# Nine pairs of mixer projections by seven block products, and weight remainders by accumulating transfers

## The chip, the cores and the metric

The kernel runs on one core of a Trainium2 chip. The metric is the device time of one execution in microseconds (us). A profiled execution has its own time, and a span from its first to its last instruction. The engines are called as in the profile: PE (TensorE matmul), PEld (its weight loads), DVE (VectorE), ACT (ScalarE), POOL (GpSimd) and SP (SyncE, which issues transfers here).

## The reference

Two post-norm layers over 528 tokens (512 and 16 meta tokens) of 1024 features, all in float32:

```python
def hybrid_mixer(h, w_in, q_norm_g, kv_norm_g, w_uq, w_ukv, w_out, pos, valid):
    proj = h @ w_in
    sb_q, sb_k, sb_v, c_q, c_kv, k_r, r_q, r_k, r_v, r_g = jnp.split(proj, IN_SPLITS, axis=-1)
    out_a = stick_breaking_attention(hs(sb_q, SB_HEADS), hs(sb_k, SB_HEADS), hs(sb_v, SB_HEADS), valid)
    q = (rms_norm(c_q, q_norm_g) @ w_uq) ...
    kv = (rms_norm(c_kv, kv_norm_g) @ w_ukv) ...
    out_b = mla_attention(q_nope, q_rope, k_nope, k_rope, v_b, valid)
    rq, rk = apply_rope(hs(r_q, 4), pos), apply_rope(hs(r_k, 4), pos) * (RET_QK ** -0.5)
    y_c = head_norm(multiscale_retention(rq, rk, hs(r_v, 4))).reshape(B, L, D_RET)
    out_c = silu(r_g) * y_c
    return jnp.concatenate([out_a, out_b, out_c], axis=-1) @ w_out

for l in range(DEPTH):
    mix = hybrid_mixer(h, ...)
    h = layer_norm(DN_ALPHA * h + mix, ln1_g[l], ln1_b[l])
    h = layer_norm(DN_ALPHA * h + jnp.square(jax.nn.relu(h @ w_ff1[l])) @ w_ff2[l], ln2_g[l], ln2_b[l])
```

`w_in` has 30 blocks of 128 output features here: 12 for stick-breaking attention (four head pairs of q, k, v), four for retention's q and k (numbers 12 to 15), eight for its values and gates (16 to 23), and six for the latents of the latent attention (24 to 29, the last the rotary key).

## The kernel before, in words

Features lie on partitions, tokens in columns. Every operand of a matmul is a pair of fp32r tiles: `hi`, the rounded value, and `lo`, the remainder. A product is three matmuls, hi*hi, hi*lo and lo*hi, added up in PSUM (`proj`, L650). A block of 128 outputs over K = 1024 is eight tiles of K, so 24 matmuls for each group of columns. Two groups of columns, 256 and 272, cover 528 tokens; in layer 1, whatever only queries need (retention's q, the gates, the query latents) is one group of 512.

Weights come through `wload` (L536): SP loads 128x512 into one of eight raw tiles (pool `r`), ACT copies it to `hi`, and DVE subtracts to get `lo` (`wsplit`, L549; 14 tiles in pool `w`). The MLP's matmuls use another scheme, `strassen` (L630): two weight blocks and two halves of K form a 2x2 matrix, the two halves of the tokens another, and seven block products of four K tiles each (84 matmuls) give what eight would (96). Its weight side (`strassen_weights`, L558) makes seven split weight tiles, of which two are sums that a transfer adds up while it lands (issued by POOL) and two are sums that DVE adds. Its other side, `strassen_sums` (L593), makes sums of the token halves.

`ret_qk` (L972) projects retention's q and k and applies rotation; `ret_vg` (L1028) makes one head's values and its gate; `mla_c` (L1123) makes the latents and norms them; `mla_proj` (L1186) takes them to heads; `wout_part` (L1320) is one of the 12 pieces of the output projection (group 0 stick-breaking, 1 retention, 2 latent attention).

The order on each engine comes from a planner (`schedule`, L312): every operation is recorded with a rank, and a list scheduler with estimated costs places it on its engine when its operands are due and its tiles are free; the table `PR` holds the ranks. PE gets the matmuls of projections as filler between the steps of the attention chains. The pool `u` holds 75 tiles of 528 columns.

Of the kernel before, what the change touches and what calls it, by code (L numbers as in the profile page):

```python
# [425 lines left out]
class Builder:  # L426
# [109 lines left out]
    def wload(self, src, eng=None):  # L536
# [3 lines left out]
        for c in range(0, n, 512):  # L540
# [4 lines left out]
            hi, lo = self.wsplit(raw, eng)  # L545
# [12 lines left out]
    def strassen_weights(self, src1, src2):  # L558
# [55 lines left out]
    def strassen_inputs(self, a, b, H, i):  # L614
# [13 lines left out]
        return d  # L628

# [94 lines left out]
    def ln_emb(self, h, c0, c1):  # L724
# [6 lines left out]
        self.ln_back(xns, 0, h, c0, c1)  # L731
# [1011 lines left out]
```

## Time and profile before

| | |
|---|---|
| median of 3 runs | 1547.27 us (1546.6 to 1547.67) |
| the profiled execution's own time | 1546.99 us |
| its span | 1545.2 us |
| PE busy | 1504.6 us (97%), 11490 matmuls |
| PEld busy | 1443.6 us (93%) |
| DVE, ACT, POOL busy | 1303.8, 963.7, 197.9 us |
| granted PE clock, mean | 0.995 |

The stages in order of time, by the shapes and places of their instructions: start and first norm until about 30 us; layer 0's stick-breaking attention with its projections 30 to 130; retention and the latents, with the last stick-breaking heads, 130 to 300; latent attention 300 to 410; end of the mixer, norm and the plain part of the MLP 410 to 480; MLP 480 to 770; norm 770 to 810; then layer 1 in the same order, 810 to 905, 905 to 1058, 1058 to 1163, 1163 to 1229, 1229 to 1510, and the last norm and output. All operations are recorded through one helper and have one line, L414, so that groups are told apart by tiles and shapes: `w` weights, `r` raw weights, `u` everything else in SBUF, `ps` PSUM, `t` small statistics.

### The profile page before, as it was taken

What the parts mean: (1) busy time and instruction counts of PE and PEld (TensorE: products, weight loads), DVE (VectorE), ACT (ScalarE), POOL (GpSimd) and SP (SyncE); (2) the same over time, 40 slices, a digit from 0 to 9 for tenths busy, and PEclk for the clock granted to TensorE, in tenths of its full rate; (3) what the DMA queues carried; (4) which work ended last, traced back from release to release, by engine and by line L of the source; (5) the groups of instructions that cost most, each with busy time, mean ns of one, the idle gap of its engine ahead of it and who ended that gap; (6) DMA issues with size and microseconds to landing.
All of it is one profiled execution on the core that took longest, in us unless ns stands there. A gap on an engine that the chain in (4) does not pass through costs nothing.

```text
span 1545.2 us, 31629 instructions
## 1 busy us (share of the span) xinstructions
PE 1504.6 (97%) x11490; PEld 1443.6 (93%) x11490; DVE 1303.8 (84%) x3131; ACT 963.7 (62%) x2263; POOL 197.9 (13%) x309
## 2 busy tenths in 40 slices
PE   6999999999999999999999999999999999999997
PEld 6999999988999999999999999888889899999996
DVE  7778877998789898888877778779987988989896
ACT  5675744578667484757646657446884857666670
POOL 4113100010001111111102112001000011111110
PEclk9999999999999999999999999999999999999999
DMA  5424412321124767677514333424212277777752
GB/s 196 117 78 124 141 62 76 100 81 49 56 83 115 185 165 178 177 181 175 171 56 131 103 91 95 127 76 125 57 62 83 69 190 180 186 183 181 186 154 82
DMA packets 102668, 190.32 MB, mean 123 GB/s; under 512 B 13552, under 2 KB 14832, under 8 KB 102512
## 3 DMA queue, kind: packets, MB, share of 16 engines
q1 hardware_dynamic: 81840, 145.98, 30.0%
q0 software_dynamic: 20672, 42.32, 14.9%
q8 instruction: 90, 1.47, 0.4%
q14 instruction: 66, 0.54, 0.1%
HBM read 167.87 MB, written 2.10 MB: 110 GB/s over the span
## 4 chain that ended last, share of the span: by engine, by line
PE 87%; DVE 9%; ACT 2%; issue 1%; DMA 0%; SPq 0%; DVEq 0%; ACTq 0%
PE ps L414 87%; DVE u L414 6%; ACT u L414 2%; DVE t L414 2%; DVE w L414 1%; DMA u<-in_xm 0%; SPq L414 0%; DVE r L414 0%; ACT w L414 0%; DVEq L1738 0%; ACT t L414 0%; DVEq L414 0%; ACTq L414 0%
## 5 line engine op out<-in xcount | busy, mean ns | idle before, releaser
L414 PE MATMUL ps<-u,w 128*128 128x256 f32 (+3 forms) x9384 | 1281.2, 294 | 14.7 <-DVE u L414 7.6
L414 PEld LDWEIGHTS ps<-u,w 128*128 128x128 f32 x9384 | 1199.7, 189 | 49.7 <-DVE u L414 11.3
L414 ACT CAST w<-r 128x512 fp32r<-128x512 f32 x610 | 364.5, 617 | 293.0 <-PE ps L414 249.2
L414 DVE TENSOR_TENSOR w<-r,w 128x512 fp32r<-128x512 f32 x604 | 404.8, 686 | 59.2 <-ACT w L414 42.9
L414 DVE TENSOR_TENSOR u<-u,u 128x512 fp32r<-128x512 f32 (+10 forms) x541 | 283.3, 548 | 10.8 <-ACT u L414 8.9
L414 DVE TENSOR_TENSOR u<-ps,u 128x256 fp32r<-128x256 f32 (+11 forms) x518 | 198.0, 409 | 48.3 <-ACT u L414 28.8
L414 PE MATMUL ps<-u,u 128*128 128x272 f32 (+5 forms) x1012 | 183.8, 307 | 1.7 <-ACT u L414 0.9
L414 POOL DMA_DIRECT2D r<-in_wff x108 | 94.8, 881 | 652.0 <-DVE u L414 331.4
L414 ACT CAST u<-u 128x512 fp32r<-128x512 f32 (+7 forms) x287 | 149.8, 540 | 39.9 <-DVE u L414 34.7
L414 ACT ACTIVATE u<-u 128x256 f32<-128x256 f32 (+5 forms) x349 | 161.7, 475 | 15.3 <-DVE u L414 12.3
L414 PEld LDWEIGHTS ps<-u,u 128*128 128x128 f32 (+1 forms) x1012 | 150.2, 190 | 8.6 <-ACT u L414 1.4
L414 ACT ACTIVATE u<-ps 128x512 f32<-128x512 f32 (+9 forms) x185 | 88.6, 484 | 89.8 <-PE ps L414 78.6
L414 DVE TENSOR_TENSOR u<-u,ps 128x256 f32<-128x256 f32 (+3 forms) x236 | 98.7, 429 | 43.6 <-PE ps L414 42.3
L414 POOL DMA_DIRECT2D u<-u x112 | 58.0, 523 | 483.7 <-ACT u L414 442.6
L414 PE MATMUL ps<-ident,u 128*128 128x128 f32 x672 | 103.4, 278 | 12.4 <-DVE t L414 9.2
L414 ACT COPY u<-ps 128x256 f32<-128x256 f32 (+6 forms) x186 | 72.1, 395 | 54.3 <-PE ps L414 52.2
L414 PEld LDWEIGHTS ps<-ident,u 128*128 128x128 f32 x672 | 79.7, 142 | 19.1 <-DVE t L414 7.9
L414 ACT CAST u<-ps 128x16 fp32r<-128x16 f32 (+7 forms) x260 | 72.4, 330 | 26.4 <-PE ps L414 15.8
L414 DVE TENSOR_TENSOR r<-r,r 128x512 f32<-128x512 f32 x108 | 74.0, 685 | 2.3 <-DMA r<-in_wff 2.1
L414 DVE SCALAR_TENSOR_TENSOR u<-ps,u 128x512 f32<-128x512 f32 (+7 forms) x73 | 41.6, 579 | 25.5 <-ACT u L414 23.2
L414 ACT ACTIVATE u<-ps,t 128x512 f32<-128x512 f32 (+4 forms) x86 | 48.0, 561 | 16.7 <-DVE t L414 13.5
L414 DVE CAST u<-u 128x256 fp32r<-128x256 f32 (+5 forms) x147 | 49.6, 353 | 8.2 <-ACT u L414 7.7
(57 smaller groups left out, 600.6 us busy)
## 6 DMA issues: line engine op xcount, KB each, us to landing
r<-in_wff SPq DMA_DIRECT2D x310, 256.0 KB, 3.3
r<-in_win SPq DMA_DIRECT2D x120, 256.0 KB, 3.0
r<-in_wff POOLq DMA_DIRECT2D x108, 256.0 KB, 4.8
r<-in_wout SPq DMA_DIRECT2D x48, 256.0 KB, 2.9
u<-u POOLq DMA_DIRECT2D x80, 132.0 KB, 4.0
u<-u SPq DMA_DIRECT2D x48, 66.0 KB, 2.4
u<-in_xm SPq DMA_DIRECT2D x10, 256.0 KB, 5.5
u<-in_dec SPq DMA_DIRECT2D x8, 264.0 KB, 3.5
```

The costliest lines, as they stand in the source:

```text
L414: o.ins = getattr(getattr(nc, o.eng), o.fn)(*[r(x) for x in o.args], **{k: r(x) for k, x in o.kw.items()})
```

## The change

Three things are done. (1) Nine pairs of blocks in each layer (retention's q and k, four heads' value with gate, and three pairs of latents) go through `strassen` in a new `pair_proj`, with halves of 264 tokens in both layers; the token side is made once per layer by `right_factors`, from the unsplit activations `raw`, which are now kept. (2) For the stick-breaking weights of head pairs 1 to 3, `mla_proj`, two groups of the output projection and one of the seven weights of each pair, `lo` is made by `wsplit_dma`: ACT writes the negative rounded weight, and a second transfer, issued by POOL, adds the weight to it. (3) Ranks move: output projection group 0 later, the latents ahead of retention's last heads. `strassen_weights` also loads and splits `a12` before `a11`, in the MLP too.

```diff
-    wo0=(1.6, 1.6), mc=(7.9, 6.8), mp0=(7.4, 7.0), ...
+    wo0=(3.1, 3.1), mc=(6.8, 6.0), mp0=(7.2, 6.8), ... hs=(2, 2), hp=2, ...
+    def wsplit_dma(self, raw, src):
+        hi, lo = self.W.tile([P, n], F32R), self.W.tile([P, n], F32R)
+        with nc.rank(nc.cur + PR['wl']):
+            nc.scalar.activation(lo, raw, AF.Copy, scale=-1.0)
+            nc.gpsimd.dma_start(lo, src.bitcast(F32R), accum_op=ALU.add)
+            nc.scalar.copy(hi, raw)
...
-    def strassen_weights(self, src1, src2):
+    def strassen_weights(self, src1, src2, dma=False):
         load("s1", a21, a22)
+        load("a12", a12)
         load("a11", a11)
-        load("a12", a12)
         w["s1"] = self.wsplit(t["s1"])
+        single = lambda n, src: self.wsplit_dma(t[n], src) if dma else self.wsplit(t[n])
+        w["a12"] = self.wsplit(t["a12"])
         w["a11"] = self.wsplit(t["a11"])
...
-        w["a12"] = self.wsplit(t["a12"])
         w["s3"] = self.wsplit(t["s3"])
-        w["a22"] = self.wsplit(t["a22"])
+        w["a22"] = single("a22", a22)
+    def right_factors(self, h, raw, H, keep=False):
+        for i in range(4):
...
+            self.strassen_sums(raw[i], raw[i + 4], t1[:, o], e[:, :H], t)
+            self.split(th[:, :2 * H], tl[:, :2 * H], t[:, :2 * H], "a")
+            self.split(t2[0][:, o], t2[1][:, o], e[:, :H], "a")
...
+            if keep:
+                self.split(*hs[i]["t1"], t1[:, o], "a")
+    def pair_proj(self, src1, src2, hs):
+        w = self.strassen_weights(src1, src2, True)
+        c1, c2 = self.unit(), self.unit()
+        self.strassen(w, hs, ("z1", "y", "x1", "z2", "x2", "x3", "x4"), H, dict(
+            z1=lambda X, Y, Z: nc.scalar.copy(c2[:, B], Z), y=lambda X, Y, Z: nc.scalar.copy(c1[:, A], Y),
+            x1=lambda X, Y, Z: nc.vector.tensor_add(c1[:, A], X, c1[:, A]),
+            z2=lambda X, Y, Z: nc.scalar.copy(c1[:, B], Z),
+            x2=lambda X, Y, Z: nc.vector.tensor_add(c1[:, B], X, c1[:, B]),
+            x3=lambda X, Y, Z: nc.vector.scalar_tensor_tensor(out=c2[:, B], in0=X, scalar=-1.0, in1=c2[:, B], op0=ALU.mult,
+                                                              op1=ALU.subtract),
+            x4=lambda X, Y, Z: nc.scalar.activation(c2[:, A], X, AF.Copy, scale=-1.0)))
+        return c1, c2
     def sb_weights(self, l, p, ranks=None):
+                ws.append(self.wload(self.a["win"][l, 3 * p + i], (self.nc.gpsimd if i in PR['GW'] else None) if ranks else
+                                     "dma" if p else None))
     def ret_qk(self, l, hs):
-                self.proj(pa[:, :n], wa, 0, h, c0, c1)
-                self.proj(pb[:, :n], wb, 0, h, c0, c1)
+            pa, pb = self.pair_proj(self.a["win"][l, 12 + 2 * which], self.a["win"][l, 13 + 2 * which], hs)
     def ret_vg(self, l, hd, hs):
-        V = last(self.v_tokens(wv, 0, h, 1))
+        v, g = self.pair_proj(self.a["win"][l, 16 + 2 * hd], self.a["win"][l, 17 + 2 * hd], hs)
+        V = self.v_parts(v, 1)
     def mla_c(self, l, hs):
+        ckv = self.pair_proj(win(27), win(28), hs)
+        cq = self.pair_proj(win(24), win(25), hs)
+        c3, kt = self.pair_proj(win(26), win(29), hs)
-                    nc.vector.tensor_copy(cs[i][:, c0:c1], ps[:, :n])
     def mla_proj(self, l, p, cn, kr, tabs):
-        wq = self.wload(self.a["wuq"][l, p])
-        wkv = self.wload(self.a["wukv"][l, p])
+        wq = self.wload(self.a["wuq"][l, p], "dma")
+        wkv = self.wload(self.a["wukv"][l, p], "dma")
     def wout_part(self, l, g, c, mixed, r, h=None):
+        w = self.wload(self.a["wout"][l, g, c], "dma" if g < 2 else None)
     def layer(self, l, h, raw, first):
+            if p == PR['hp']:
+                with nc.rank(R + PR['hs'][l]):
+                    hs = self.right_factors(h, raw, NT // 2, True)
```

How this moves instructions is shown at three places. The first is PE in layer 1, where retention head 2's value and gate are projected. Before, the value is projected alone and group by group (`ps_14338` ends the group of 256 columns, `ps_14390` begins that of 272; `ps_14397` is the attention of head 0):

```order
L414 MATMUL ps_14338<-u_11939,w_14184 128x256
L414 MATMUL ps_14338<-u_11949,w_14184 128x256
L414 MATMUL ps_14338<-u_11939,w_14235 128x256
L414 MATMUL ps_14390<-u_11866,w_14062 128x272
L414 MATMUL ps_14390<-u_11877,w_14062 128x272
L414 MATMUL ps_14397<-u_14378,u_13689 128x144
L414 MATMUL ps_14390<-u_11866,w_14213 128x272
```

Now, at the same head:

```order
L414 MATMUL ps_14707<-u_12024,w_14583 128x264
L414 MATMUL ps_14707<-u_12036,w_14583 128x264
L414 MATMUL ps_14707<-u_12024,w_14596 128x264
L414 MATMUL ps_14707<-u_12079,w_14583 128x264
L414 MATMUL ps_14716<-u_13222,w_14498 128x264
L414 MATMUL ps_14716<-u_13319,w_14498 128x264
L414 MATMUL ps_14716<-u_13222,w_14521 128x264
```

The value and the gate are computed together, by products of 264 columns (`ps_14716` is the product of the first weight sum with a sum of token halves, `ps_14707` that of `a12`), and their weights come from a pair's seven sets.

The second place is DVE in layer 0, where retention's head 0 starts (`r` and `w` rows are weights, `ps` with `u_2647` or `u_2871` the decay of the scores). Before:

```order
L414 TENSOR_TENSOR w_2774<-r_2148,w_2700 128x512
L414 TENSOR_TENSOR u_2604<-ps_2693,u_2740 64x512
L414 TENSOR_TENSOR w_2796<-r_2283,w_2787 128x512
L414 TENSOR_TENSOR u_2815<-u_2604,u_2800 128x528
L414 TENSOR_TENSOR w_2825<-r_2311,w_2807 128x512
L414 TENSOR_TENSOR u_2828<-ps_2805,u_2828 128x128
L414 TENSOR_TENSOR u_2842<-ps_2835,u_2647 128x512
```

Now:

```order
L414 TENSOR_TENSOR w_2890<-r_2691,w_2793 128x512
L414 TENSOR_TENSOR u_2668<-ps_2851,u_2894 64x16
L414 TENSOR_TENSOR u_2858<-ps_2728,u_2858 128x264
L414 TENSOR_TENSOR w_2913<-r_2693,w_2897 128x512
L414 TENSOR_TENSOR w_2922<-r_2720,w_2906 128x512
L414 TENSOR_TENSOR u_2668<-ps_2845,u_2894 64x512
L414 TENSOR_TENSOR r_2935<-r_2693,r_2725 128x512
L414 TENSOR_TENSOR u_2949<-ps_2931,u_2871 128x512
```

Between the same steps of the attention now stand more splits, a weight sum (`r_2935`) and a sum read from PSUM (`u_2858<-ps_2728`).

The third place is POOL in layer 0, behind its set-up, where it copies head pair 0's q and k to the layout of the scores (`u<-u`, 64x528). Before:

```order
L414 CAST rep_434<-u_106 128x128
L414 DMA u_544<-u_313 64x528
L414 DMA u_544<-u_341 64x528
L414 DMA u_577<-u_383 64x528 x2
L414 DMA u_610<-u_313 64x528
L414 DMA u_610<-u_341 64x528
L414 DMA u_644<-u_383 64x528 x2
L414 DMA u_796<-u_656 64x528
```

Now:

```order
L414 CAST rep_434<-u_106 128x128
L414 DMA w_347<-in_win 128x512
L414 DMA w_499<-in_win 128x512
L414 DMA w_523<-in_win 128x512
L414 DMA u_548<-u_313 64x528
L414 DMA u_548<-u_341 64x528
L414 DMA u_578<-u_381 64x528 x2
L414 DMA u_615<-u_313 64x528
L414 DMA u_615<-u_341 64x528
L414 DMA u_646<-u_381 64x528 x2
L414 DMA w_542<-in_win 128x512
L414 DMA w_565<-in_win 128x512
```

Three of head pair 1's `lo` transfers stand ahead of the copies and three behind them, on the one queue of POOL.

## Rows read from the trace of the kernel before

**Rows 1.** The page, parts 1 and 2: engines' busy times, PE by slices.

```profile
PE 1504.6 (97%) x11490; PEld 1443.6 (93%) x11490; DVE 1303.8 (84%) x3131; ACT 963.7 (62%) x2263; POOL 197.9 (13%) x309
...
PE   6999999999999999999999999999999999999997
```

**Rows 2.** The page, part 4: chain that ended last, by engine.

```profile
PE 87%; DVE 9%; ACT 2%; issue 1%; DMA 0%; SPq 0%; DVEq 0%; ACTq 0%
```

**Rows 3.** Stretches: us; PE, PEld, DVE, ACT, POOL busy (instructions); clock, DMA, GB/s.

```profile
30.00:130.00 100.00, 99.46 (x775) 96.81 (x776) 76.91 (x173) 66.92 (x144) 21.34 (x40) 1.00 0.41 108
130.00:300.00 170.00, 169.95 (x1365) 168.11 (x1364) 137.22 (x351) 91.09 (x212) 10.74 (x16) 1.00 0.30 92
300.00:410.00 110.00, 106.57 (x815) 99.42 (x814) 100.89 (x357) 86.93 (x284) 11.24 (x32) 1.00 0.24 70
480.00:770.00 290.00, 283.42 (x2293) 281.09 (x2293) 258.49 (x503) 185.32 (x396) 46.81 (x55) 0.99 0.69 176
...
905.00:1058.00 153.00, 152.98 (x962) 137.92 (x961) 118.36 (x271) 81.03 (x170) 11.47 (x16) 1.00 0.33 98
1058.00:1163.00 105.00, 104.74 (x641) 90.12 (x640) 95.20 (x299) 83.14 (x252) 8.79 (x22) 1.00 0.25 71
1229.00:1510.00 281.00, 276.21 (x2293) 272.98 (x2293) 254.17 (x502) 183.79 (x396) 44.65 (x51) 0.99 0.70 176
```

**Rows 4.** The same view: PE at 264 columns, at 512, and at 256.

```profile
600.00:660.00 60.00, 60.00 (x493) 59.88 (x492) 52.45 (x101) 41.30 (x92) 10.50 (x12) 1.00 0.69 171
1213.00:1228.00 15.00, 15.00 (x67) 12.18 (x66) 14.92 (x38) 12.95 (x28) 0.87 (x1) 1.00 0.28 60
1260.00:1320.00 60.00, 60.00 (x511) 60.00 (x510) 53.20 (x106) 40.45 (x91) 10.97 (x13) 1.00 0.75 189
```

**Rows 5.** Groups by form: xcount, busy us, mean ns, idle before, releasers.

```profile
L414 DVE TENSOR_TENSOR w<-r,w 128x512 fp32r<-128x512 f32 x596 | 401.7, 690 | 59.1 <-ACT w L414 42.9 <-PE ps L414 8.4
L414 ACT CAST w<-r 128x512 fp32r<-128x512 f32 x602 | 361.5, 619 | 292.4 <-PE ps L414 248.7 <-DVE r L414 25.5 <-issue 11.2
...
L414 POOL DMA_DIRECT2D r<-in_wff x108 | 94.8, 881 | 652.0 <-DVE u L414 331.4 <-DVE w L414 110.8 <-DMA r<-in_wff 95.6
...
L414 DVE TENSOR_TENSOR r<-r,r 128x512 f32<-128x512 f32 x108 | 74.0, 685 | 2.3 <-DMA r<-in_wff 2.1
...
L414 POOL DMA_DIRECT2D u<-u x112 | 58.0, 523 | 483.7 <-ACT u L414 442.6 <-PE ps L414 19.6 <-DVE u L414 10.3
...
L414 DVE TENSOR_TENSOR u<-u,u 128x528 fp32r<-128x528 f32 x64 | 45.2, 711 | 2.6 <-ACT u L414 2.5
...
L414 DVE TENSOR_TENSOR u<-ps,u 128x264 f32<-128x264 f32 x39 | 16.7, 429 | 4.0 <-PE ps L414 3.6
...
L414 ACT COPY u<-ps 128x264 f32<-128x264 f32 x39 | 14.4, 370 | 3.2 <-PE ps L414 3.1
```

**Rows 6.** DVE in order of time: start us, us, three splits merged.

```profile
1235.29 1.89 DVE L414 TENSOR_TENSOR w<-r,w 128x512 fp32r<-128x512 f32 x3
```

**Rows 7.** Who waited for whom: us in total, times, longest.

```profile
PE ps L414 <- DVE u L414: 10.9, 16, 2.0
...
ACT w L414 <- DMA r<-in_win: 0.4, 2, 0.3
...
PEld ps L414 <- DVE w L414: 0.4, 2, 0.2
```

**Rows 8.** DMA issues: queue, xcount, KB each, median us to landing.

```profile
r<-in_win SPq DMA_DIRECT2D x120, 256.0 KB, 3.0
r<-in_wff POOLq DMA_DIRECT2D x108, 256.0 KB, 4.8
```

More of the change, by code (lines that the diff above doesn't have):

```diff
@@ L762, in v_tokens, with v_parts @@
                 yield
+        return self.v_parts(vt, heads)
+    def v_parts(self, vt, heads):
+        nc = self.nc
         n = 2 * P
@@ L1334, in wout_group, with accum, layer @@
         self.proj(ps[:, :n], w, 4 * m, mixed, c0, c1)
-        self.accum(ps[:, :n], r[mt][:, c0:c1], h[mt] if g == 0 else None, c0, c1)
-    def accum(self, ps, r, hp, c0, c1):
-        nc = self.nc
-        if hp is None:
-            nc.vector.tensor_add(r, r, ps)
-        else:
-            hi, lo = f32(hp[0][:, c0:c1]), f32(hp[1][:, c0:c1])
-            nc.vector.scalar_tensor_tensor(out=r, in0=hi, scalar=ALPHA, in1=ps, op0=ALU.mult, op1=ALU.add)
-            nc.vector.scalar_tensor_tensor(out=r, in0=lo, scalar=ALPHA, in1=r, op0=ALU.mult, op1=ALU.add)
-    def layer(self, l, h, first):
+        self.accum(ps[:, :n], r[mt][:, c0:c1], [x[:, c0:c1] for x in h[mt]] if h else ())
+    def accum(self, ps, r, h=()):
+        add = ps
+        for x in h:
+            self.nc.vector.scalar_tensor_tensor(out=r, in0=f32(x), scalar=ALPHA, in1=add, op0=ALU.mult, op1=ALU.add)
+            add = r
+        if not h:
+            self.nc.vector.tensor_add(r, r, ps)
+    def layer(self, l, h, raw, first):
         nc = self.nc
@@ L1535, in layer @@
                 ff1(mt, *g)
-        sums = []
-        for i in range(4):
-            if i % 2 == 0:
-                t1 = self.unit()
-                t2 = [self.unit(F32R), self.unit(F32R)]
-            o = slice((i % 2) * H, (i % 2) * H + H)
-            t, e = self.unit(), self.unit()
-            self.strassen_sums(raw[i], raw[i + 4], t1[:, o], e[:, :H], t)
-            th, tl = self.unit(F32R), self.unit(F32R)
-            self.split(th[:, :2 * H], tl[:, :2 * H], t[:, :2 * H], "a")
-            self.split(t2[0][:, o], t2[1][:, o], e[:, :H], "a")
-            (ah, al), (bh, bl) = h[i], h[i + 4]
-            A, B = slice(0, H), slice(H, 2 * H)
-            hs.append(dict(b11=(ah[:, A], al[:, A]), b21=(bh[:, A], bl[:, A]), b22=(bh[:, B], bl[:, B]), t1=(ah[:, B], al[:, B]),
-                           t2=(t2[0][:, o], t2[1][:, o]), t3=(th[:, A], tl[:, A]), t4=(th[:, B], tl[:, B])))
-            sums.append((hs[i]["t1"], t1[:, o]))
-        for (hi, lo), x in sums:
-            self.split(hi, lo, x, "a")
+        hs += self.right_factors(h, raw, H)
         for i in range(npl):
@@ L1577, in layer @@
         hn = None if final else self.new_h()
+        raw = None if final else [self.unit() for _ in range(KT)]
         with nc.rank(R + 31):
-            self.ln_group(r, 2, hn, *gs[0], final)
+            self.ln_group(r, 2, hn, *gs[0], final, raw)
         first = None
@@ L1585, in layer @@
         with nc.rank(R + 33):
[L1586 removed]
+            self.ln_group(r, 2, hn, *gs[1], final, raw)
         self.PP = self.PA
         nc.cur = R + 100
[L1589 removed]
+        return hn, raw, first
     def record(self):
@@ L1596, in record @@
         nc.cur = -2.6
-        self.ln_emb(h, *gs[0])
+        raw = [self.unit() for _ in range(KT)]
+        self.ln_emb(h, *gs[0], raw)
         WR = PR['WR']
@@ L1606, in record @@
         for l in range(DEPTH):
-            h, first = self.layer(l, h, first)
+            h, raw, first = self.layer(l, h, raw, first)
     def build(self):
```

158 lines of the change are left out of this document (74 added, 84 removed).

## Prediction

> **What bounds the kernel now.** I read the page's busy times first. PE is busy 1504.6 of 1545.2 us, in every slice but the first and the last nearly all of it [rows 1], and the chain that ended last runs through PE for 87% [rows 2]. A busy PE need not be a PE at its peak, so the second view is the stretches [rows 3] beside stretches of one shape of matmul [rows 4]. In the MLP 493 matmuls of 264 columns fill 60 us, 0.1217 us each; 511 of 256 columns fill 60 us, 0.1174 us each; 67 of 512 columns fill 15 us, 0.224 us each (a little too low, since those under way at an edge count too). The time follows the columns, 0.46 ns a column at 256 and 264, at a granted clock of 1.00, which is the 2.4 GHz level. What is worth something is therefore fewer columns, as long as nothing keeps PE waiting. In retention with the latents PE hardly waits: 0.05 us in 170, and 0.02 in 153 in layer 1 [rows 3]. DVE is the next engine: 81% and 77% there, 92% in layer 0's latent attention, where PE idles 3.4 us of 110, and 89 to 90% in the MLPs, where PE idles 6.6 of 290 and 4.8 of 281 [rows 3]. These say how much DVE may do before PE feels it.
>
> The sum is made against the profiled execution's own time, 1546.99 us: its span of 1545.2 and 1.8 around it. The median of the runs shown, 1547.27, is 0.02% above, so nothing is added for that. A measurement can tell about 0.2% from no change, 3.1 us: faster means below 1544.2, slower above 1550.4.
>
> **PE columns.** A pair of blocks was 2 x 24 matmuls per column group: with groups of 256 and 272, 48 x 528 = 25,344 columns; with one group of 512, 24,576. It becomes 84 matmuls of 264, 22,176 columns. In layer 0 all nine pairs have the two groups. In layer 1 nine of the 18 blocks do and nine are 512 wide. Together 648 matmuls of 256, 648 of 272 and 216 of 512 go, and 1512 of 264 come: in columns 342,144 + 110,592 - 399,168 = 53,568 fewer. At 0.46 ns that is 24.6 us, 13.1 in layer 0 and 11.5 in layer 1. With the 512-wide ones at their own 0.224 and the 272-wide ones at 0.125 (272 x 0.46 ns), it is 76.1 + 81.0 + 48.4 - 184.0 = 21.5. I take 24, since 0.224 is too low at its edges, and keep 21.5 to 24.6. The number of matmuls, and so of weight loads, stays exactly what it was: 1512 out, 1512 in.
>
> The Trainium skill, Perfetto Trace Analysis, section Identifying the Most-Contended Engine, says that TensorE's room is to be judged by the busy share of its weight loads and not by that of its matmuls; here that is 93%. If weight loads set the pace, an unchanged number of them would give back nothing; the 512-wide row speaks against that, and it is a rival below.
>
> **DVE.** Each of the nine pairs of a layer had four splits on DVE and now has six and two weight sums, so four operations of 128x512 more, and three sums that read 264 columns from PSUM. Their durations are 0.69 and 0.43 us [rows 5], but three splits in a row take 1.89 [rows 6], so 0.60 each and 0.09 of tail that the next one covers. Without tails a pair adds 4 x 0.60 + 3 x 0.34 = 3.4 us, nine 30.8. Eight splits of the output projection leave the same stretch (4.8), and the copies of the latents out of PSUM, ten of about 0.34 in layer 0 (3.4), about as much in layer 1 (four and three wide ones, 3.2). That is +22.6 a layer, on 137.2 in layer 0 and 118.4 in layer 1 [rows 3]. The right factors are four times four sums of 264 columns, one split of 528 (0.71, so 0.62) and two of 264: 10.7 us, due before the first pair, beside the stick-breaking heads, where 18 splits (10.8 us) leave DVE. So they cost nothing there; if they ran late, PE would wait for the first pair only.
>
> In the stretch of retention DVE would then have 160 us of work in 170 - 13 = 157, and 141 in 153 - 11.5 = 141.5. That is an upper bound: busy time holds the tails of instructions that nothing followed, at most 0.09 for each of about 396 and 316 instructions, 36 and 28 us. Its demand lies between 124 and 160 of 157 (79 to 102%), and between 113 and 141 of 141.5 (80 to 100%). The middle, 142 and 127, is 90%, the share of the MLPs and of latent attention. What PE idles at that share is 0.25% (layer 1's latent attention) to 3.1% (layer 0's) [rows 3]. For 298 us that is 0.7 to 9.2 us; I take 1.7%, the lower of the two MLPs, 5 us, since the MLP has this very code with the same 14 weight tiles.
>
> **ACT.** Each pair adds four operations of 128x512 at 0.53 (0.62 less tail) and four copies of 264 columns out of PSUM at 0.28 [rows 5], which take over from copies and squares that read PSUM: 9 x 3.2 = 29 us, and 4 for the output projection, on 91 in layer 0's retention [rows 3]: 124 of 157, 79%. The 18 stick-breaking weights add 9.5 us and the right factors 4.6 to 67 of 100. In latent attention 20 weight tiles add about 10 us to 87, 88% of 110, while DVE loses about 11 of its 101. One engine is relieved and the other loaded, so I count the 3.4 us that PE idles there as unchanged; all of it could go, or as much again come.
>
> **POOL, SP and the transfers.** POOL gets 146 more transfers: 92 for single weights, and for each of 18 pairs one `lo` and two weight sums. At 0.52 to 0.88 us [rows 5] that is 76 to 128 us on an engine that is busy 198 of 1545, and SP issues 18 more. Nothing of it lies on the path, because weights are ready early: ACT waited 0.4 us in all for projection weights to land, and weight loads 0.4 for DVE's splits [rows 7]. A `lo` by transfer comes about 5 us later than by DVE: 4.8 to land [rows 8] and 0.9 to issue, against 0.7. The DMA share of 0.30 in that stretch rises, but the MLP lives with 0.69 [rows 3]. In POOL's queue a transfer that waits for ACT holds up the copies of q and k behind it, and the stick-breaking scores wait for those: cost nothing while ACT is ahead, and else the rival below.
>
> **The latents earlier.** Their norm chain now runs beside retention's last heads and not ahead of latent attention. What it can save is in the 3.4 us above. The order of `a12` and `a11` in the MLP shifts one split by about 0.6 us in a stream that is prepared ahead (the 0.4 us of weight loads behind DVE's splits [rows 7] holds for the MLP too). I count nothing.
>
> **Sum:** 1547.0 - 24 + 5 = **1528 us**. With 24.6, no new idle time and the 3.4 gone it is 1519; with 21.5, 9.2 and 3.4 more it is 1538. Its own range is 1518 to 1535, the sum's ends not all coming together.
>
> **The rivals.** (a) *DVE becomes the bound of retention.* No stretch shows DVE above 92%. At the top of its demand the two stretches last 160/0.92 = 174 and 141/0.92 = 153 us, not 157 and 141.5: 29 us more, 1547 - 24 + 29 = 1552, slower than before. It decides from a demand of 92% on (145 and 130 us); halfway from there to the top it costs 9 and 6 us, 1547 - 24 + 15 = 1538. For it: DVE waits on PE and ACT between the steps of attention, which the MLP has less of. Against it: the right factors and some weights can be made ahead, and the middle of the demand stays below. Chance: 0.17 for a part (1535 to 1544), 0.06 for above that.
>
> (b) *The accumulating transfers come late.* A layer has 30 sets of weights that use them: nine stick-breaking blocks, four second latent projections, eight pieces of the output projection and nine pairs. One that PE must wait for costs up to the 5 us above; eight of them are 40 us: 1547 - 24 + 40 = 1563. It takes six to make the kernel slower. Against it is the 0.4 us of waits [rows 7]; for it, that one queue holds splits and copies together. Chance 0.05.
>
> (c) *Weight loads set the pace*, and 1512 of them for 1512 give nothing: 1547, no change. Against it: one load took 0.224 us of pace at 512 columns and 0.117 at 256 [rows 4]. Chance 0.04.
>
> (d) Below 1518, should the shorter DVE work beside stick-breaking attention and latent attention give more than I see: 0.04.
>
> **How the numbers follow.** Forecast 0.64 (1518 to 1535), (a) 0.17 and 0.06, (b) 0.05, (c) 0.04, (d) 0.04. Faster: 0.64 + 0.17 + 0.04 = 0.85. Above 1544.2, (a) and (b) leave 0.01 each within the bound, so with (c) 0.06 the same, and 0.09 slower. The range 1518 to 1544 holds 0.81.
>
> **What would show it.** Right: 11490 matmuls again and PE busy about 1480; PE idle in retention below 5 us a layer; DVE busy 87 to 95% there and about 1325 in all; POOL busy some 300. Wrong by (a): PE's waits on DVE, 10.9 us now [rows 7], go to 40 and more, in retention. Wrong by (b): weight loads wait for `w` from a transfer. Wrong by (c): the same span with PE's pace at 264 columns as slow as at 272.

## The result, and the profile after

The changed kernel is slower: 1561.94 us, median of four runs (1560.68 to 1567.92), against 1546.93 (1546.33 to 1547.67) for the kernel before in the same comparison. The ratio is 1.0106, with a 95% interval of 1.0089 to 1.0123. Forecast were 1528 and a range up to 1544.

The profiled execution took 1560.68 us, its span 1558.9. The page, parts 1, 2 and 4 (busy times, PE by slices, the chain by engine), against [rows 1] and [rows 2]:

```profile
PE 1495.7 (96%) x11490; PEld 1435.1 (92%) x11490; DVE 1324.1 (85%) x3172; ACT 1061.6 (68%) x2485; POOL 325.7 (21%) x449
...
PE   6999999899999999999999998999999999999997
...
PE 79%; DVE 11%; ACT 3%; DMA 3%; issue 2%; POOL 0%; SPq 0%; DVEq 0%; ACTq 0%; POOLq 0%
```

The work is what was forecast: 11490 matmuls, DVE at 1324.1 us (1325), POOL at 325.7 (some 300). PE's busy time fell by 8.9 us where 24 were due, and its idle time (span less busy) rose from 40.6 to 63.2. The stretches, with the columns of [rows 3]:

```profile
30.00:130.00 100.00, 96.77 (x753) 93.76 (x753) 73.22 (x176) 76.81 (x169) 38.25 (x58) 1.00 0.66 147
130.00:300.00 170.00, 164.17 (x1279) 158.52 (x1277) 151.26 (x363) 119.62 (x268) 44.97 (x54) 1.00 0.72 171
300.00:410.00 110.00, 104.80 (x773) 96.44 (x772) 94.33 (x334) 89.18 (x282) 22.67 (x45) 0.97 0.43 99
480.00:770.00 290.00, 285.34 (x2309) 283.15 (x2308) 261.80 (x510) 189.81 (x407) 46.19 (x55) 0.99 0.69 173
905.00:1058.00 153.00, 145.88 (x1044) 137.87 (x1043) 133.08 (x299) 104.92 (x227) 41.09 (x47) 0.98 0.70 167
1058.00:1163.00 105.00, 101.90 (x623) 87.36 (x622) 88.12 (x267) 88.38 (x259) 27.59 (x44) 0.98 0.57 130
```

PE idles 5.8 and 7.1 us in the two stretches of retention, where it had idled 0.05 and 0.02; 5.2 and 3.1 in latent attention (3.4 and 0.3); 3.2 beside the stick-breaking heads (0.5). The MLP is as before. The windows keep their times while the work slides by some us, so these are sums for a region and not for the same instructions. Finer cuts, same columns, find where in it:

```profile
160.00:180.00 20.00, 18.12 (x135) 16.72 (x135) 16.86 (x34) 13.98 (x30) 8.58 (x12) 1.00 0.78 200
200.00:280.00 80.00, 80.00 (x648) 79.38 (x648) 68.81 (x189) 49.80 (x110) 15.62 (x18) 1.00 0.67 156
280.00:300.00 20.00, 17.71 (x135) 16.41 (x134) 16.07 (x44) 18.23 (x50) 6.94 (x8) 1.00 0.94 221
300.00:320.00 20.00, 17.36 (x104) 15.27 (x104) 18.39 (x58) 9.94 (x26) 7.48 (x15) 0.83 0.73 178
...
940.00:960.00 20.00, 17.82 (x132) 16.15 (x131) 17.09 (x33) 13.34 (x29) 5.14 (x5) 1.00 0.72 181
960.00:980.00 20.00, 16.53 (x90) 15.09 (x89) 16.53 (x34) 15.49 (x34) 8.04 (x12) 0.83 0.85 186
980.00:1060.00 80.00, 80.00 (x587) 76.48 (x586) 69.22 (x172) 54.49 (x120) 16.24 (x19) 1.00 0.69 165
```

In the long middle of retention PE is full. The loss sits at two places of each layer: where retention's first pairs run beside the last stick-breaking block (130 to 200 and 905 to 980 us), and where the latents are finished (280 to 320 and 1060 to 1100 us). The same windows before:

```profile
160.00:180.00 20.00, 20.00 (x161) 19.66 (x160) 16.34 (x38) 15.42 (x36) 4.74 (x10) 1.00 0.63 180
300.00:320.00 20.00, 19.20 (x141) 17.27 (x140) 19.77 (x67) 11.34 (x32) 5.82 (x16) 1.00 0.42 108
960.00:980.00 20.00, 19.98 (x116) 17.29 (x115) 14.04 (x27) 9.07 (x19) 3.21 (x7) 1.00 0.73 215
980.00:1060.00 80.00, 80.00 (x488) 71.49 (x487) 63.87 (x161) 37.97 (x81) 2.04 (x4) 1.00 0.28 85
```

At both places the granted clock fell as well (0.83 at 300 to 320 and at 960 to 980 us, 1.00 before). Over the whole span its mean went from 0.995 to 0.991. An us at the lower level (1.2 GHz) gives half the work of one at 2.4, so the mean stands for 14.0 us of full-speed work lost against 7.7. Some 4 us of either are the last 7 to 8 us of the span, where the clock is low and PE has nothing left to do; while PE is busy, 9.6 us are lost against 3.4. That is 6 us of the 15 missing in PE's busy time. The other 9 were not traced: they may be waits too short to show as idle, or the columns may be worth less than 24 us (the prediction's own low price makes them 21.5).

Who waited for whom (us in total, times, longest), against [rows 7]:

```profile
PE ps L414 <- DVE u L414: 18.6, 31, 1.5
PE ps L414 <- ACT u L414: 11.6, 15, 2.8
...
PE ps L414 <- DMA w<-in_win: 2.6, 2, 1.9
...
PEld ps L414 <- DMA w<-in_win: 4.5, 6, 2.1
...
PEld ps L414 <- DMA w<-in_wukv: 1.8, 2, 1.1
```

### The profile page after: what moved, and what is told of

The parts are those of the page before. It is cut to its first block, busy times and chain, and to the rows that moved or that the text cites. A ratio compares the mean times of both kernels' runs of the same rounds, so it can differ in the third digit from the quotient of the medians.

```text
span 1558.9 us, 32237 instructions
## 1 busy us (share of the span) xinstructions
PE 1495.7 (96%) x11490; PEld 1435.1 (92%) x11490; DVE 1324.1 (85%) x3172; ACT 1061.6 (68%) x2485; POOL 325.7 (21%) x449
## 4 chain that ended last, share of the span: by engine, by line
PE 79%; DVE 11%; ACT 3%; DMA 3%; issue 2%; POOL 0%; SPq 0%; DVEq 0%; ACTq 0%; POOLq 0%
PE ps L414 79%; DVE u L414 8%; ACT u L414 3%; DMA w<-in_win 2%; DVE t L414 1%; DVE w L414 1%; ACT w L414 1%; DVE r L414 1%; DMA w<-in_wukv 0%; DMA u<-u 0%; DMA u<-in_xm 0%; SPq L414 0%; POOL u L414 0%; DMA r<-in_wout 0%; POOL w L414 0%
## 5 line engine op out<-in xcount | busy, mean ns | idle before, releaser
L414 PE MATMUL ps<-u,w 128*128 128x264 f32 (+3 forms) x9384 | 1261.4, 291 | 24.1 <-DVE u L414 10.7
L414 ACT CAST w<-r 128x512 fp32r<-128x512 f32 (+1 forms) x664 | 396.7, 616 | 260.0 <-PE ps L414 212.5
L414 DVE TENSOR_TENSOR u<-u,u 128x512 fp32r<-128x512 f32 (+12 forms) x591 | 314.9, 558 | 15.7 <-ACT u L414 13.9
L414 DVE TENSOR_TENSOR u<-ps,u 128x264 f32<-128x264 f32 (+14 forms) x510 | 193.0, 406 | 52.2 <-ACT u L414 29.4
L414 ACT CAST u<-u 128x512 fp32r<-128x512 f32 (+6 forms) x305 | 159.1, 543 | 36.6 <-DVE u L414 30.8
L414 ACT ACTIVATE u<-u 128x256 f32<-128x256 f32 (+7 forms) x362 | 172.0, 487 | 14.7 <-DVE u L414 12.1
L414 PE MATMUL ps<-ident,u 128*128 128x128 f32 x672 | 104.0, 277 | 13.2 <-DVE t L414 10.3
L414 ACT ACTIVATE u<-ps 128x432 f32<-128x432 f32 (+9 forms) x174 | 81.8, 481 | 47.3 <-PE ps L414 44.6
L414 ACT COPY u<-ps 128x264 f32<-128x264 f32 (+5 forms) x224 | 85.8, 392 | 38.4 <-PE ps L414 36.8
L414 POOL DMA_DIRECT2D w<-in_win x54 | 48.5, 935 | 218.1 <-ACT w L414 79.0
L414 ACT ACTIVATE w<-r 128x512 fp32r<-128x512 f32 (+1 forms) x110 | 68.2, 620 | 19.3 <-PE ps L414 12.6
```

Source lines behind the costliest of these rows:

```text
L414: o.ins = getattr(getattr(nc, o.eng), o.fn)(*[r(x) for x in o.args], **{k: r(x) for k, x in o.kw.items()})
```

## The experiments

Eighteen kernels ran; each ratio is to runs of the kernel before on the same chip (medians of 1545.1 to 1546.9 us). "+" is the median less that of before beside it; the clock is the mean granted to the profiled execution.

| kernel | median us | + | ratio [95%] | span, PE busy | clock |
|---|---|---|---|---|---|
| the change | 1561.94 | 15.0 | 1.0106 [1.0089, 1.0123] | 1558.9, 1495.7 | 0.991 |
| e1 no low parts by transfer | 1575.53 | 30.0 | 1.0191 [1.0174, 1.0209] | 1573.1, 1501.5 | 0.985 |
| e2 before, low parts by transfer | 1555.28 | 9.8 | 1.0059 [1.0044, 1.0074] | 1551.0, 1504.1 | 0.996 |
| e3 change, old ranks | 1570.84 | 25.3 | 1.0163 [1.0148, 1.0178] | 1569.5, 1501.5 | 0.986 |
| e4 before, new ranks | 1546.88 | 1.4 | 1.0007 [0.9997, 1.0016] | 1543.9, 1501.1 | 0.997 |
| e5 e1, pairs' low parts left out | 1554.08 | 9.0 | 1.0055 [1.0042, 1.0068] | 1553.7, 1494.6 | 0.989 |
| e6 change, stick-breaking on DVE | 1559.04 | 13.9 | 1.0093 [1.0079, 1.0108] | 1561.2, 1499.1 | 0.984 |
| e7 before, three pairs a layer | 1555.28 | 10.2 | 1.0063 [1.0047, 1.0080] | 1556.7, 1505.3 | 0.990 |
| e8 before, right factors unused | 1549.65 | 4.5 | 1.0032 [1.0020, 1.0044] | 1551.5, 1508.8 | 0.992 |
| e9 change, factors early | 1562.24 | 16.0 | 1.0107 [1.0090, 1.0125] | 1559.4, 1498.7 | 0.987 |
| e10 change, latents as before | 1553.33 | 7.1 | 1.0048 [1.0031, 1.0065] | 1551.8, 1494.9 | 0.993 |
| e11 retention pairs | 1548.57 | 2.3 | 1.0015 [1.0005, 1.0025] | 1546.1, 1494.9 | 0.993 |
| e12 e7, factors early | 1549.61 | 3.3 | 1.0024 [1.0014, 1.0033] | 1546.6, 1497.8 | 0.994 |
| e13 e5, one tile a weight | 1561.12 | 15.2 | 1.0096 [1.0080, 1.0111] | 1560.1, 1498.5 | 0.985 |
| e14 change, 18 weight tiles | 1538.69 | -7.2 | 0.9961 [0.9946, 0.9976] | 1536.7, 1485.1 | 0.992 |
| e15 pairs in layer 0 alone | 1537.92 | -8.0 | 0.9951 [0.9939, 0.9964] | 1536.1, 1493.0 | 0.996 |
| e16 e15, fewer transfers | 1542.22 | -3.7 | 0.9978 [0.9970, 0.9987] | 1542.6, 1496.2 | 0.996 |
| e17 e15, 18 weight tiles | 1523.09 | -22.2 | 0.9850 [0.9835, 0.9865] | 1519.0, 1486.5 | 0.997 |
| e18 before, 18 weight tiles | 1524.60 | -20.7 | 0.9867 [0.9850, 0.9883] | 1521.7, 1491.1 | 0.997 |

### Which part costs: e1 to e4

The first theory was the transfers (T); the rivals were the pairs themselves (P, later D) and the moved latents (M).

```diff
 # e1: the changed kernel
-        wq = self.wload(self.a["wuq"][l, p], "dma")
+        wq = self.wload(self.a["wuq"][l, p])
...
-        w = self.strassen_weights(src1, src2, True)
+        w = self.strassen_weights(src1, src2)
 # e3: the changed kernel; e4: the same line the other way, in the kernel before
-    wo0=(3.1, 3.1), mc=(6.8, 6.0), mp0=(7.2, 6.8), ...
+    wo0=(1.6, 1.6), mc=(7.9, 6.8), mp0=(7.4, 7.0), ...
```

e2 puts `wsplit_dma` into the kernel before, at the changed kernel's single weights.

> The changed kernel, with every low part of a weight made on DVE again (no accumulating transfer for a low part; the weight sums of the pairs stay). Theory T (the transfers of low parts cost the time: they stand in POOL's queue ahead of the copies of q and k): the gain in columns comes through, 1526 to 1540 us, and the copies of q and k land in about 4 us again instead of 6.3. Rival P (the pairs' own vector work and hand-overs cost it): 1555 to 1575, since 110 splits of 0.6 us (66 us) come back to DVE, with PE's waits on DVE above the 18.6 us of the changed kernel. Rival M (the new order of the latents costs it): as the changed kernel, 1555 to 1565, with the idle time at 280 to 320 us unchanged.

> The kernel before, with nothing changed but the low parts of the single weights, made by accumulating transfers in the same 92 places as in the changed kernel. T: slower than before by 8 to 25 us (1555 to 1572), with idle time of PE behind w<-in_win and behind the copies of q and k. P and M: within 4 us of before (1543 to 1551), since PE had no wait for these weights.

> The changed kernel with the old ranks of the output projection's first group, of the latents and of the first latent pair (the order of before). M: 1540 to 1548, the idle time at 280 to 320 us and 1060 to 1100 us gone (about 9 us with the low clock). T and P: 1556 to 1568, the idle time of the stretches with retention's projections (130 to 200, 905 to 980) the same or more.

> The kernel before with the new ranks and nothing else. M: slower than before by 5 to 15 us (1552 to 1562). T and P: 1543 to 1550.

T fell as the main cause: without those transfers the kernel is not faster but 15 us slower than the change (e1). They do cost by themselves (e2, +9.8). Its waits, and its DMA issues (queue, KB each, median us to landing):

```profile
PE ps L414 <- DMA w<-in_win: 3.5, 3, 1.5
```

```profile
u<-u POOLq DMA_DIRECT2D x80, 132.0 KB, 6.6
w<-in_win POOLq DMA_DIRECT2D x36, 256.0 KB, 7.3
```

The copies of q and k, which stand in the same queue, land in 6.6 us there, in 6.3 in the change, in 4.0 before, and in 3.0 in e1, which makes no low part by transfer. PE idled 4.7 us of 100 beside the stick-breaking heads in e2 (0.5 before). So they cost there, and next to the pairs they pay, since they take 60 us off DVE. M fell as well: the new ranks alone do nothing (e4), and in the changed kernel they save 10.3 us (e3). What is left is the pairs. With every low part made on DVE, as before (e1), they cost 30 us with the move, although the columns are fewer. e1 came out just above P's range, e2 at the lower edge of T's, e3 above both of its own; only e4 lies clearly in one, that of T and P.

### What in the pairs: e5, e8, e6 and e7

```diff
 # e5: e1, in the pairs' weights
             nc.scalar.copy(hi, raw)
-            (eng or nc.vector).tensor_sub(lo, raw, f32(hi))
+            nc.gpsimd.memset(f32(lo), 0.0)
 # e8: the kernel before with, at p == 2,
+                with nc.rank(R + PR['hs'][l]):
+                    hs = self.right_factors(h, raw, NT // 2, True)
```

> The kernel of e1 (pairs, no accumulating transfer for a low part) in which the low parts of the pairs' weights are left out: POOL writes zeros into their tiles, early and with nothing to wait for, in place of seven differences a pair on DVE. The products, the tiles and their lifetimes stay. That takes 126 x 0.6 = 76 us from DVE, nearly all of it in the stretches of retention and the latents. Theory D (the pairs load DVE until PE waits for it there, and what PE waits lowers its clock): 1522 to 1540, DVE below 85% at 130 to 200 and 905 to 980 us, and no stretch below a granted clock of 0.97. Rival L (the pairs cost by their longer chain of hand-overs, three sums over PSUM and later results, whatever DVE's load): 1555 to 1575, like e1.

> The kernel before with the right factors computed in each layer and used by nothing: 16 sums and 16 splits on DVE, 16 casts on ACT a layer, beside the stick-breaking heads. What the prediction counted at nothing. If that was right: 1544 to 1550. If they delay the heads' own steps: 1550 to 1558.

e5 lies between its theories. DVE is busy for 75 us less, and 21.0 of e1's 30.0 come back, so DVE is part of it. But 9.0 us and what the columns are worth (33, if that is 24) stay lost with DVE busy for only 56 of 70 and 54 of 75 us. Its stretches, columns as above:

```profile
130.00:200.00 70.00, 68.70 (x522) 66.80 (x521) 56.23 (x122) 50.86 (x109) 31.17 (x48) 0.98 0.58 152
...
280.00:320.00 40.00, 31.40 (x216) 28.89 (x215) 38.59 (x115) 23.38 (x67) 5.23 (x14) 0.87 0.39 113
...
905.00:980.00 75.00, 70.03 (x483) 64.69 (x482) 54.36 (x111) 49.90 (x105) 30.04 (x47) 0.95 0.54 140
```

These shares are means too. At 280 to 320 us DVE is full, and so it is in the 15 us of the last stretch in which most of PE's idle time lies. In 5 us each, e5:

```profile
945.00:950.00 5.00, 3.40 (x28) 2.96 (x26) 3.22 (x8) 4.83 (x11) 1.37 (x3) 1.00 0.59 215
950.00:955.00 5.00, 4.01 (x27) 3.49 (x28) 5.00 (x7) 4.44 (x10) 3.70 (x3) 1.00 0.45 80
955.00:960.00 5.00, 4.32 (x27) 3.24 (x25) 5.00 (x10) 3.69 (x9) 2.18 (x4) 1.00 0.78 175
960.00:965.00 5.00, 3.30 (x12) 2.67 (x13) 5.00 (x13) 2.90 (x6) 2.56 (x6) 0.69 0.80 204
```

In the change DVE is busy for 19.96 of 20 us at 950 to 970 us, where PE idles 4.8. A full DVE alone does not stop PE: before, at 950 to 960 us, in the same part of layer 1,

```profile
950.00:955.00 5.00, 5.00 (x40) 4.91 (x40) 4.98 (x13) 3.57 (x8) 0.00 (x0) 1.00 0.09 32
955.00:960.00 5.00, 5.00 (x40) 4.92 (x39) 4.97 (x10) 2.67 (x6) 2.79 (x4) 1.00 0.21 50
```

both are full. So e5 excludes DVE's mean share as the measure, and not DVE in the 15 us that matter. Nor is e5 a pure removal: its zeros on POOL waited 168.8 us in all for PE to give weight tiles back, and what follows in POOL's queue stood behind them.

e8 shows that the right factors, counted at nothing, cost 4.5 us (3.1 to 6.8 by the interval). Its time of 1549.65 lies inside the range written for nothing; the kernel before beside it took 1545.1. They add 28 operations on DVE and 12 on ACT a layer, not 16 sums, 16 splits and 16 casts. DVE runs most of layer 0's in one go from 107.7 to 117.9 us, ahead of the attention of the third stick-breaking block and of the weights that follow. The stretches behind it, 5 us each:

```profile
115.00:120.00 5.00, 5.00 (x41) 4.77 (x40) 4.91 (x13) 4.13 (x9) 2.65 (x6) 1.00 0.55 158
120.00:125.00 5.00, 4.06 (x31) 3.44 (x29) 4.97 (x12) 4.56 (x13) 1.45 (x3) 1.00 0.83 207
125.00:130.00 5.00, 4.32 (x19) 4.09 (x19) 4.23 (x10) 3.44 (x9) 0.00 (x1) 0.63 0.84 273
130.00:135.00 5.00, 5.00 (x21) 4.68 (x22) 3.59 (x7) 3.17 (x6) 2.25 (x4) 0.50 0.02 8
135.00:140.00 5.00, 5.00 (x35) 4.86 (x36) 3.69 (x10) 1.30 (x3) 0.00 (x0) 0.85 0.17 52
140.00:145.00 5.00, 5.00 (x41) 4.91 (x40) 4.96 (x13) 1.65 (x3) 0.00 (x0) 1.00 0.16 52
```

PE idles 1.6 us, 1.0 behind ACT and 0.6 behind DVE, and then its clock is at 0.63, 0.50 and 0.85 for 15 us, of which 5.1 us of full-speed work are lost (5 x 0.37 + 5 x 0.50 + 5 x 0.15), with PE shown as busy: 21 matmuls in 5 us, not 41. This execution took 1553.33 us, 3.7 above the kernel's median, so the stall need not be as long in the others.

> The changed kernel with the low parts of the 18 stick-breaking blocks on DVE again, where it has room (73 of 100 us); all other transfers as they are. Theory T (those transfers are late there): 1550 to 1557, the 2.7 us of PE idle at 30 to 130 us and 2.5 at 770 to 840 us gone. Theory D: no help at 905 to 980 us, or worse, since eleven microseconds of splits a layer come back to DVE and the last of them stand at its door: 1558 to 1568.

> The kernel before with pairs for three of the nine only: values and gates of retention's heads 1 to 3, which run at 200 to 280 us and 980 to 1060 us, where PE did not idle in the changed kernel; right factors as in the changed kernel; no accumulating transfer for a low part, old ranks. 16,704 fewer columns, 7.7 us at 0.46 ns. Theory D: 1538 to 1545, faster than before by 0 to 8 us, because DVE has room in these stretches (63 and 64 of 80 us) for 10 us more. Rival L: slower than before, 1550 to 1556.

e6 passes `None` for `"dma"` in the stick-breaking blocks; e7 is the kernel before with pairs for retention's heads 1 to 3 alone. e6 cannot be told from the change (the intervals overlap): PE's idle at 770 to 840 us fell from 2.5 to 0.5 us, but at 905 to 980 us, where DVE has the splits again, PE was busy for 66.25 of 75 at a clock of 0.87 (67.88 in the change). The execution profiled was the slowest of its four.

e7 speaks for L and against D: three pairs a layer, in stretches where PE stayed full (79.87 of 80 and 80 of 80), cost 10.2 us, 4.5 of them the factors' of e8 by that kernel's measure, though 17,856 columns went. Both stretches behind the factors ran at a lower clock again:

```profile
130.00:200.00 70.00, 69.59 (x514) 67.79 (x513) 57.52 (x123) 40.45 (x89) 17.02 (x24) 0.94 0.42 107
905.00:980.00 75.00, 73.00 (x461) 66.15 (x461) 60.42 (x121) 42.91 (x88) 17.18 (x23) 0.95 0.45 118
```

This execution is the slowest of six. They run from 1550.42 us at a mean clock of 0.996 to 1558.5 at 0.990.

### Undoing one by one: e9 to e12

```diff
 # e9: the changed kernel
-    ... hs=(2, 2), hp=2, ...
+    ... hs=(2.75, 2.75), hp=1, ...
 # e10: the changed kernel with mla_c and the ranks of the kernel before
-                    cn, kr = self.mla_c(l, hs)
+                    cn, kr = self.mla_c(l, h)
```

e11 is e9 and e10 with e6's edit; e12 is e7 with e9's edit.

> The changed kernel with the right factors recorded one stick-breaking block earlier and at a rank behind that block's own steps (hp 1, hs 2.75), so that they fill DVE's free time from about 50 us on in place of a run of some 10 us at 106 to 117 us. Theory F (the factors in one run delay the third block's steps; e8 showed 4.5 us for them): 1554 to 1559, and the stalls of the stick-breaking heads at 100 to 130 us and 900 to 910 us smaller. Theory D or L (what the pairs bring later costs the time, the factors little beside it): 1560 to 1566.

> The changed kernel with the latents made as in the kernel before (24 matmuls a block and group, old ranks), so six pairs a layer and not nine. PE gets 7.7 us of columns back. Theory L (the norms of the latents can start only when whole pairs of blocks are done; the idle time and the low clock at 280 to 320 and 1080 to 1100 us are theirs, 10.6 us idle and 5 of clock): 1550 to 1558, granted clock 1.00 at 280 to 320 us. Theory D (DVE's load in all): 1566 to 1574, since the columns come back and DVE is relieved only where it was not full.

> e9 and e10 together, and the stick-breaking weights' low parts on DVE: pairs for retention alone, factors early, transfers of low parts for the second latent projections, the output projection and the pairs' last block. F and L: 1541 to 1551, what each takes away adding up. D: 1555 to 1565, with DVE above 92% and PE idle 5 us and more at 130 to 200 and at 905 to 980 us.

> e7 (three pairs a layer, values and gates of heads 1 to 3, no transfers of low parts) with the factors early as in e9. F: 1541 to 1549, e7 less the 4.5 us of the factors and less the low clock at 130 to 200 and 905 to 980 us (about 4 us each). D or L: 1552 to 1558, as e7.

e10 settles the latents' share. With their three pairs a layer and their move taken back the kernel is 7.9 us faster, though 17,856 columns return, 8.2 us at 0.46 ns: they cost near 16 where they should have given 8. The change at 280 to 320 us, then e10:

```profile
280.00:320.00 40.00, 35.07 (x238) 31.68 (x238) 34.46 (x101) 28.17 (x75) 14.42 (x23) 0.91 0.83 199
```

```profile
280.00:320.00 40.00, 39.16 (x315) 38.24 (x313) 33.75 (x100) 26.73 (x69) 15.37 (x26) 1.00 0.85 191
```

DVE is hardly less busy in e10 and the DMA share no lower. In the change PE waited there 2.4 us on ACT and 1.2 on DVE, by the chain for casts and splits of the normed latents (the tiles are all `u`), and 0.9 for a transfer of `w`. That the norms start later because they need whole pairs fits this chain; no run tries it by itself. The chain of waits over this stretch of the changed kernel (start us, us, what):

```profile
280.00 12.11 PE ps L414 x99
...
295.91 6.60 DVE u L414 x17
...
303.00 1.69 DVE u L414 x4
...
304.74 5.36 PE ps L414 x25
```

The factors' place (e9) is worth nothing in the whole change, and 6.9 us where little else stalls (e12 against e7). F holds for them alone, and their stall is covered by others in the change. e11 comes to +2.3: six pairs a layer are worth less than they cost, still. e9 fell in the range of D and L, e10 in L's, e11 in that of F and L, e12 just above F's.

### Weight tiles, and layer 0 alone: e13 to e18

A pair takes 14 weight tiles, and there are 14. Theory W put the rest on that.

```diff
 # e13: e5 with one tile a weight
-        hi, lo = self.W.tile([P, n], F32R), self.W.tile([P, n], F32R)
+        hi = self.W.tile([P, n], F32R)
...
+        return hi, hi
 # e14, e17, e18: the changed kernel, e15, the kernel before
-        self.U = Pool(self.sb, "u", NT, 75).stream(75)
-        self.W = Pool(self.sb, "w", 512, 14).stream(14)
+        self.U = Pool(self.sb, "u", NT, 71).stream(71)
+        self.W = Pool(self.sb, "w", 512, 18).stream(18)
 # e15: e11, and in layer 1 the kernel before's
+                    rst = self.ret_qk(l, hs) if full else self.ret_qk_old(l, h)
```

> e5 with one tile for each of a pair's weights instead of two: no tile is set aside for the low part (left out), and its products read the tile of the high part. DVE's and ACT's work as in e5, a pair holds 7 of the 14 weight tiles instead of all 14. Theory W (a pair holds every weight tile, so the next weights come late): 1535 to 1546, the idle time of PE at 130 to 200 us and 905 to 980 us (e5: 1.3 and 5.0 us, and a granted clock of 0.98 and 0.95) mostly gone. Rival S (the dependent steps of the stick-breaking block and of the latents' norms set the end, with fewer columns to fill them): 1550 to 1557, as e5.

> The changed kernel with 18 weight tiles in place of 14, and 71 tiles for activations in place of 75. W: 1545 to 1556. S or D: 1558 to 1568, no better, or worse from the fewer tiles for activations.

> e11 in layer 0 (six pairs for retention, factors early, latents as before), and layer 1's projections as in the kernel before; transfers of low parts for the second latent projections and the output projection of both layers. The first layer of e11 ended 5.5 us ahead of the kernel before, its second was 9.8 us longer up to the MLP. So: 1540 to 1545, faster than before by 2 to 6 us. If the second layer's loss came from the transfers and not from its pairs: 1546 to 1551.

> e15 without the transfers of low parts of the second latent projections and of the output projection (the pairs' last block keeps its own). If those transfers relieve DVE without being late: 1543 to 1549, slower than e15. If they are late in both layers: 1538 to 1543, faster than e15.

By the time alone e14 would have proved W: 1538.69 us. Its profile says otherwise. The stretch beside the last stick-breaking block and the MLP, in e14:

```profile
480.00:770.00 290.00, 289.84 (x2379) 289.42 (x2378) 261.43 (x509) 188.05 (x404) 46.31 (x55) 1.00 0.71 178
...
905.00:980.00 75.00, 65.22 (x446) 61.23 (x446) 63.91 (x120) 47.12 (x98) 22.10 (x27) 0.93 0.61 156
```

Retention is no better than in the change (PE 67.88 of 75 there); the gain is in the MLP, with 2379 matmuls in 290 us for 2309. e13, which frees half of a pair's tiles, is 6 us slower than e5, and PE idles no less there:

```profile
130.00:200.00 70.00, 66.83 (x491) 64.41 (x491) 55.02 (x116) 48.48 (x103) 18.25 (x23) 0.95 0.58 145
905.00:980.00 75.00, 69.56 (x501) 65.14 (x500) 58.33 (x118) 53.23 (x113) 18.22 (x24) 0.98 0.60 154
```

So W falls for retention. That calls for a control, the kernel before with the same tiles:

> e15 with 18 weight tiles and 71 tiles for activations. If the four tiles work in the MLPs alone, their 18 to 23 us come off e15: 1515 to 1522. If they only mend what the pairs had spoilt: 1530 to 1538.

> The kernel before with 18 weight tiles and 71 tiles for activations, nothing else. If the gain of e14 has nothing to do with the change: 1522 to 1530, with PE's lost time in the MLPs gone. If it is the pairs' weight tiles that it serves: 1542 to 1550.

The stretches of the MLPs in e18, against [rows 3]:

```profile
480.00:770.00 290.00, 289.90 (x2384) 289.57 (x2383) 258.61 (x506) 185.98 (x398) 46.81 (x55) 1.00 0.70 177
...
1229.00:1510.00 281.00, 280.87 (x2380) 280.41 (x2379) 251.09 (x505) 172.94 (x374) 42.89 (x49) 1.00 0.68 174
```

91 and 87 more matmuls in the same time, at 0.1217 us each [rows 4], are 21.7 us; the kernel gained 20.7. 11.1 of them are idle time that is gone, and most of the rest is pace, 0.1216 us a matmul for 0.1236. The gain is the MLPs' own and has nothing to do with the change. The Trainium skill, Perfetto Trace Analysis, section Optimization Strategy, takes a bubble that keeps returning on the engine that should be full as a possible sign of too few buffers; the MLPs' 6.6 and 4.8 us of idle, now 0.1 each, agree.

e15 is the best without it, 8.0 us faster than before: pairs for retention in layer 0 alone, with early factors, and low parts by transfer for the second latent projections and the output projection of both layers. The stretch at 905 to 980 us with pairs in layer 1 (e11), then without (e15):

```profile
905.00:980.00 75.00, 68.24 (x452) 62.33 (x451) 60.51 (x116) 49.37 (x104) 22.61 (x28) 0.93 0.64 156
```

```profile
905.00:980.00 75.00, 74.85 (x493) 68.16 (x493) 53.97 (x120) 44.21 (x94) 14.70 (x18) 1.00 0.48 132
```

Layer 1's six pairs with their right factors cost 10 us net (e11 less e15). e16 splits e15's 8.0: without those transfers 3.7 are left, which are the pairs', and 4.3 are the transfers'. e16 is slower than e15, as its first theory had it, just under that theory's range. With the tiles, e17 is the fastest at 1523.09, but e18 with 1524.60 and an overlapping interval cannot be told from it: on top of them, layer 0's pairs are not shown to give anything. Of the ranges written, e13 came out above both, e14 and e15 below theirs, e17 just above that of the tiles working in the MLPs alone, and e18 in that of a gain that has nothing to do with the change.

## Why the prediction was wrong

**Right:** the number of matmuls, DVE's and POOL's busy time, DVE's share in retention (89 and 87%, 87 to 95 forecast), and the count of columns: by the shapes of the matmuls 53,568 went. At 980 to 1060 us, where PE never idled, 587 matmuls ran in the time of 488, with 165,616 columns for 168,128, which speaks against rival (c). What the columns are worth was not confirmed in full.

**The miss by terms:** the span was to be 1526.2 us (1545.2 - 24 + 5) and was 1558.9. Of the 32.7 between, 15.1 are busy time of PE that did not go. 17.6 are more idle time than forecast: 8.0 in retention, 4.6 in latent attention, some 5 at 30 to 130 and 770 to 840 us beside the stick-breaking heads.

**The step that failed** is the one from an engine's mean share to PE's idle time: "I take 1.7%, the lower of the two MLPs, 5 us, since the MLP has this very code with the same 14 weight tiles". PE idled 13.0 us in those stretches, and e5 shows that the mean share does not set it: at 72% (54 of 75 us) PE still lost 5.0 us and ran at 0.95. A mean over 170 us hid that PE is full in the middle and stalls in a few us beside the last stick-breaking block, and that DVE is full just there. That the block's steps wait for each other, and that the pairs leave too little else for PE to do meanwhile, fits the rows and was not tried. The MLP was also the wrong measure: its idle time went with four more weight tiles (e18).

**Terms counted at nothing that were not:** the right factors, "So they cost nothing there", cost 4.5 us alone (e8). The latents, "I count the 3.4 us that PE idles there as unchanged", cost some 16 (e10); that their norms wait for whole pairs is argued. The move that the prediction also held to be worth nothing saves 10.3 with the pairs and nothing without (e3, e4). For the transfers, "Nothing of it lies on the path" failed twice: alone they cost 9.8 us (e2), and with the pairs they save 15 (e1). And **the clock** was in no term: 6 us of work more than before in the change, and 17 in e6's slowest execution ((0.995 - 0.984) x 1561).

**The rivals:** (a), DVE as the bound, is the nearest: e1 to e5 gives it 21 us, but of e1's DVE, which has more to do than the change's; the change and e5 differ by 6.0 us. Its sign came true too weakly (PE's waits on DVE 10.9 to 18.6, not 40); that the transfers had relieved DVE fits that. (b) named the time, 1563, by luck. Its sign showed weakly: weight loads waited 4.5 and 1.8 us for `w` by transfer, PE 2.6 for `in_win`, where before neither did. But without those transfers the kernel is slower (e1).

**What stays open:** why the stretch at 905 to 980 us starves in e5. DVE's mean load and the weight tiles do not explain it (e5, e13, e14). Two explanations are left, that DVE has too much to do in those 15 us and that a block of dependent steps has fewer columns to fill its waits; neither was tried by itself. Nor were the raw weight tiles, of which a pair uses seven of eight: they were never varied, and at 940 to 980 us ACT waited 5.1 us on DVE's `r` in the change. Every edit also makes the planner place all instructions anew, and no run held the order fixed, so a few us between two kernels may be the new order's. Why e13 is slower than e5, and why the pairs pay in layer 0 and not in layer 1, is open too.

## What to carry to other kernels

Do not size a stall by the mean share of an engine: cut the stretch until PE's idle time sits in one window, and ask which engine is full there, which chain of dependent steps runs, and what fills its waits. A product scheme whose results are complete only after a whole pair is to be tried place by place: in this kernel it paid 3.7 us in retention of layer 0 (e16) and cost in layer 1 and in the latents. That it belongs where no chain waits for the first result is a guess that fits these three. And let the profile say where a gain came from before it is credited: e14's came from the MLP, and the control that showed it (e18) beat the change by 36 us, each against the kernel before beside it, with two numbers.

## What the runs showed of the hardware

A short stall can cost PE twice. In e8 1.6 us of idle in 10 us were followed by 15 us at granted clocks of 0.63, 0.50 and 0.85 (means of its two levels, 1.2 and 2.4 GHz), worth 5.1 us; in the change the same happened at 300 to 320 and 960 to 980 us (0.83 each). It need not: at 160 to 180 us of the change PE idled 1.9 of 20 us and the clock stayed at 1.00. One kernel's time moves with it: e7's executions lie 8 us apart, at mean clocks of 0.996 and 0.990. The Trainium skill, TensorE: Matmul & The Clock Gate, section HAM oscillation — how this bites in real kernels, says that waits for a transfer between bursts of matmuls put the clock back to half and that the next burst pays for it; these rows agree, with waits on DVE and ACT that are spread over several us and not in one piece.
